# Sample rows through one transpose, the first weight chunk ordered by feature block, one product that spreads a norm's sums

## The chip, the cores and the metric

One core of a Trainium2 chip runs the whole kernel. The metric is the device time of one execution in microseconds (us), as the median of several runs.

## The reference

One decoder layer with 2048 features runs over 264 tokens: 256 of a prompt and one new token for each of eight samples. Everything is float32. In outline, with the details of the three branches left out:

```
xn = rmsnorm(x, norm_mix_g)                      # x * rsqrt(mean(x*x) + eps) * g
z  = xn @ w_in                                   # 2048 x 9728: gmlp, q, k, v, memory q, gates
o_g, o_a, o_m = gmlp(z), window_attention(z), memory_attention(z, mem_prompt)
merged = sum over b of sigmoid(gate_b) * (o_b @ w_br_b)
x = x + merged @ w_out
h = rmsnorm(x, norm_ffn_g) @ w_up                # 2048 x 11264
h = conv_b + sum over j of shifted h * conv_w[j]
x = x + (gelu(a) * b) @ w_down                   # a, b = the halves of h
y = rmsnorm(x, final_norm_g)
```

The change lies in the first step (x to xn, and the first product of it) and in the two places where a norm's 1/rms is worked out.

## The kernel before

**Layout.** Tokens lie along the free axis, features on the 128 partitions, so x is turned once on arrival: `xT`, 16 feature blocks of 128 x 264. A float32 operand is held as two parts of type float32r, a rounded one and the rest: `xhi` and `xlo` for x (with the gain, and without 1/rms, which is multiplied in when a product leaves PSUM), `whi` and `wlo` for the weights. One block of a product takes three matmuls (hi hi, lo hi, hi lo).

**The stream.** `gemm` writes chunks into one list. A chunk is two feature blocks of one product: its load fills `raw` (four buffers), `split` makes `whi` on ScalarE (ACT) and `wlo` on VectorE (DVE), and TensorE (PE) then does nm blocks x 2 feature blocks x 3 matmuls. `run` writes `split` ahead of use: chunk 0 alone first, then chunks 1 and 2 ahead of the matmuls of chunk 1, then one more chunk each time, and again two (5 and 6) ahead of chunk 4's. Every engine issues strictly in the order in which the code is written (`InOrder`). A slot is the work of one output block; `later(n, f)` writes f into the stream n slots on.

**x.** x arrives in eight column groups `xl`, each with two feature blocks. I call these pairs 0 to 7, and pair k feeds chunk k of the first product, q's first half (nm = 3, 18 matmuls a chunk). `x_parts(k0)` turns a pair with PE into PSUM tiles named `xtp`: four transposes of 128 x 128 and two small ones of the sample rows `xs`. ACT then writes both `xhi` and DVE both `xlo`. `x_kept` copies block one of the pair to `xT` on ACT and block two on DVE, squares them (ACT and GpSimd, called POOL), and POOL adds the squares to `ssum`. Each `xtp` before the change holds one feature block, in a PSUM tile of its own. In chunk k the pair k+1 is turned after the first output block; only pair 1 is turned ahead of chunk 0.

**Norms.** `token_norm` sums `ssum` over the partitions token by token (six small PE instructions, `ntp`), and `spread` brings 1/rms to all partitions with a product of a diagonal (`stp`). This happens for x (`r_bc`) and for the feed-forward part (`r2_bc`).

`mem_prep`, which the change leaves alone, turns two blocks of the memory rows into one PSUM tile `mtp`; ACT writes `mhi` from it and DVE `mlo`. PSUM tiles come from `psA` (`acc_t`, 4 buffers) and `psM` (`mis_t`, 4 buffers), each buffer 128 x 512 float32.

Of the kernel before, what the change touches and what calls it, by code (L numbers as in the profile page):

```python
# [39 lines left out]
class InOrder:  # L40
    """An engine whose instructions issue in the order in which they are written."""
# [19 lines left out]
def body(ctx, tc, x_prompt, x_sample, cache_swa_k, cache_swa_v, cache_mem_k, cache_mem_v, state_conv,  # L61
# [21 lines left out]
    # ---- slots: a slot is the matrix work of one output block and weight chunk; other work is  # L83
    # written into the stream at a slot, far enough behind what it needs ----
# [19 lines left out]
    def inv_sqrt(dst, v, shape):  # L104
        """Stages of dst = 1 / sqrt(v), with a step of Newton's method."""
        y = sm.tile(shape, F32, name="rs_y", tag="rs_y%d" % shape[1], bufs=2)
        t = sm.tile(shape, F32, name="rs_t", tag="rs_t%d" % shape[1], bufs=2)

        def a():
            S.activation(y, v, AF.Sqrt)  # L110

        def b():
            V.reciprocal(y, y)
            V.scalar_tensor_tensor(out=t, in0=y, scalar=-0.5, in1=y, op0=mul_, op1=mul_)
            V.tensor_tensor(t, t, v, op=mul_)
            V.scalar_tensor_tensor(out=dst, in0=t, scalar=1.5, in1=y, op0=add_, op1=mul_)
        return a, b

    def token_norm(srcs, out):
        """Stages of out[token] = 1 / rms over the features, from sums of squares over the blocks."""  # L120
        st = {}

        def a():
            tp = st["tp"] = mis_t("ntp")
            for tb in range(3):
                np_ = 128 if tb < 2 else 8
                for i, q in enumerate(srcs):
                    T.matmul(tp[:np_, tb:tb + 1], lhsT=q[:, 128 * tb:128 * tb + np_], rhs=ones[:, 0:1],
                             start=i == 0, stop=i == len(srcs) - 1)
            v = st["v"] = sm.tile([128, 3], F32, name="nv_", tag="nv_", bufs=2)  # L130
            G.memset(v, 1.0)

        def b():
            tp, v = st["tp"], st["v"]
            V.tensor_scalar(v[:, 0:2], tp[:, 0:2], 1.0 / D, EPS, op0=mul_, op1=add_)
            V.tensor_scalar(v[:8, 2:3], tp[:8, 2:3], 1.0 / D, EPS, op0=mul_, op1=add_)
            st["f"] = inv_sqrt(out, v, [128, 3])
            st["f"][0]()
        return a, b, lambda: st["f"][1]()

    def spread(r, dst):
        """Stages of dst[p, token] = r[token] for every partition p."""
        st = {}

        def a():
            dg = st["dg"] = sm.tile([128, NT], F32, name="dg", tag="sq", bufs=4)
            V.tensor_scalar(dg[:, 0:128], ident, r[:, 0:1], None, op0=mul_)
            V.tensor_scalar(dg[:, 128:256], ident, r[:, 1:2], None, op0=mul_)
            V.tensor_scalar(dg[:8, 256:264], ident[:8, :8], r[:8, 2:3], None, op0=mul_)

        def b():
# [7 lines left out]
    ident = cst.tile([128, 128], F32, name="ident")  # L159
    make_identity(nc, ident)  # L160
    ones = cst.tile([128, 128], F32, name="ones")
    G.memset(ones, 1.0)
# [12 lines left out]
    rx = cst.tile([128, 3], F32, name="rx")  # L175
# [6 lines left out]
    st_ld, st_mix, st_pb, st_me, st_gt, st_s2, st_s2p, st_s3k, st_s3v, st_s1, st_s5, st_mg = (  # L182
        ExitStack() for _ in range(12))

# [1 line left out]
    ld = st_ld.enter_context(tc.tile_pool(name="ld", bufs=1))  # L186
    xls = [ld.tile([128, 2, 256], F32, name="xl%d" % i) for i in range(8)]
    xs = ld.tile([8, D], F32, name="xs")
    gm = ld.tile([16, 128], F32, name="gm")
    grow = ld.tile([48, 128], F32, name="grow")  # L190

    def x_load(i):
        Y.dma_start(xls[i], x_prompt[0, :, 256 * i:256 * i + 256].rearrange("(t p) f -> p t f", p=128))
        if i == 0:
            Y.dma_start(gm, norm_mix_g[0].rearrange("(k p) -> k p", p=128))
            Y.dma_start(xs, x_sample[:, 0, :])
# [3 lines left out]

    def x_parts(k0):
        """Two feature blocks of x, gained and split."""
        if k0 == 0:
            tp = mis_t("gtp")
            T.transpose(out=tp[:, 0:16], in_=gm, identity=ident[:16, :16])
            V.tensor_copy(gT[:, 0:16], tp[:, 0:16])
        xl = xls[k0 // 2]
        tps = []
        for j in range(2):
            kb = k0 + j  # L210
            tp = mis_t("xtp")
            js = slice(128 * j, 128 * j + 128)
            T.transpose(out=tp[:, 0:128], in_=xl[:, 0, js], identity=ident)
            T.transpose(out=tp[:, 128:256], in_=xl[:, 1, js], identity=ident)
            T.transpose(out=tp[:, 256:264], in_=xs[:, 128 * kb:128 * kb + 128], identity=ident[:8, :8])
            tps.append(tp[:, :NT])
        for j in range(2):
            S.activation(xhi[:, k0 + j, :], tps[j], AF.Copy, scale=gT[:, k0 + j:k0 + j + 1])
        for j in range(2):
            V.scalar_tensor_tensor(out=xlo[:, k0 + j, :], in0=tps[j], scalar=gT[:, k0 + j:k0 + j + 1],  # L220
                                   in1=xhi[:, k0 + j, :], op0=mul_, op1=sub_)
        return tps

    def x_kept(k0, tps):
        S.copy(xT[:, k0, :], tps[0])
        V.tensor_copy(xT[:, k0 + 1, :], tps[1])
        sq = [sm.tile([128, NT], F32, name="sq", tag="sq", bufs=4) if k0 + j else ssum for j in range(2)]
        S.activation(sq[0], tps[0], AF.Square)
        if k0 < KB - 2:
            G.tensor_tensor(sq[1], xT[:, k0 + 1, :], xT[:, k0 + 1, :], op=mul_)  # L230
# [3 lines left out]
        if k0:  # L234
            E.tensor_tensor(ssum, ssum, sq[0], op=add_)
        E.tensor_tensor(ssum, ssum, sq[1], op=add_)
# [16 lines left out]
    def split(load, n, pairs):  # L253
# [13 lines left out]
        for r, h, l in vs:  # L267
            V.tensor_tensor(l, r, h, op=sub_)
        return list(zip(his, los))
# [28 lines left out]
    def gemm(load, nkb, nm, ab, evac, pairs=False, pre=None, mid=None, banks=None):  # L298
        """ab() gives the high and low parts of the moving operand."""
        st = {}  # L300

        def chunk(kc):
            def mm(ws):
# [4 lines left out]
                ahi, alo = ab()  # L308
                for m in range(nm):
                    o = st["acc"][m][:, :NT]  # L310
                    for j in range(2):
                        kb = 2 * kc + j
                        hi, lo = blk(ws[j][0], m), blk(ws[j][1], m)
# [1220 lines left out]
```

## Time and profile before

| | |
|---|---|
| median of 3 runs | 1548.16 us (1545.2 to 1552.09) |
| span of the profiled execution | 1546.5 us, mean granted TensorE clock 0.997 |
| PE busy | 1531.6 us, 99% |
| DVE, ACT, POOL busy | 1011.2, 768.9, 139.3 us |
| DMA | 285.57 MB, 185 GB/s |

The span runs from the first to the last instruction of one profiled execution. The profile gives no time of that execution beside its span; the span lies 1.7 us under the median of the runs. Over the whole kernel PE is busy nearly all the time, but the change touches the first 55 us and two short places later, so these have to be read by themselves.

### The profile page before, as it was taken

How to read it: one execution, taken by the hardware profiler on the slowest of the kernel's cores; microseconds unless marked ns; L12 is line 12 of the kernel's file. 1: busy time of each engine (PE TensorE's matmuls, PEld its weight loads, DVE VectorE, ACT ScalarE, POOL GpSimd, SP SyncE). 2: the span in 40 equal slices, each digit the busy share in tenths (PEclk: the TensorE clock that was granted, in tenths of full speed). 3: DMA queues.
4: the chain of work that ended last, by engine and by line, in shares of the span. 5: the costliest groups of instructions: out<-in, count | busy, mean ns of one | idle time of the engine just before them, and what ended most of it. 6: DMA issues, size and time to landing. Idle time of an engine off the chain costs nothing.

```text
span 1546.5 us, 31609 instructions
## 1 busy us (share of the span) xinstructions
PE 1531.6 (99%) x12203; PEld 1497.4 (97%) x12203; DVE 1011.2 (65%) x1934; ACT 768.9 (50%) x1492; POOL 139.3 (9%) x215
## 2 busy tenths in 40 slices
PE   9999999999999999999999999999999999999997
PEld 8987899999999999999999999999999999999997
DVE  7577678867475555765667777776444776777564
ACT  6467644565444444445555555554343555555443
POOL 5022042400000000001100000000000000001110
PEclk9999999999999999999999999999999999999998
DMA  6754498665666565555566666655556666665743
GB/s 198 213 179 153 137 309 299 219 188 159 181 182 183 180 179 180 185 172 185 178 178 179 186 182 178 180 184 182 178 180 181 185 177 179 181 184 174 185 162 111
DMA packets 154372, 285.57 MB, mean 185 GB/s; under 512 B 11509, under 2 KB 29357, under 8 KB 154165
## 3 DMA queue, kind: packets, MB, share of 16 engines
q1 hardware_dynamic: 152444, 278.14, 58.8%
q0 software_dynamic: 1776, 5.41, 1.5%
q8 instruction: 96, 1.57, 0.4%
q14 instruction: 56, 0.45, 0.1%
HBM read 279.10 MB, written 6.82 MB: 185 GB/s over the span
## 4 chain that ended last, share of the span: by engine, by line
PE 96%; DVE 1%; DMA 1%; issue 0%; ACT 0%; POOL 0%; DVEq 0%; SPq 0%; ACTq 0%; POOLq 0%
PE acc L50 88%; PE macc L50 3%; DMA raw<-in_w_down_dram 1%; PE sps L50 1%; PE ov L50 1%; DVE wlo L50 1%; PE xtp L50 1%; PE acc__552 L50 0%; PE acc__551 L50 0%; PE ssp L50 0%; PE ytp L50 0%; PE ptp L50 0%; PE mtp L50 0%; PE msov L50 0%; DMA gm<-in_norm_mix_g_dram 0%
## 5 line engine op out<-in xcount | busy, mean ns | idle before, releaser
L50 DVE TENSOR_TENSOR wlo<-raw,whi 128x512 fp32r<-128x512 f32 (+1 forms) x1008 | 658.9, 695 | 478.0 <-ACT whi L50 477.5
L50 ACT CAST whi<-raw 128x512 fp32r<-128x512 f32 (+1 forms) x1008 | 564.8, 607 | 618.5 <-PE acc L50 421.7
L50 PE MATMUL acc<-xg_hi,whi 128*128 128x264 f32 x1408 | 400.4, 284 | 0.0
L50 PE MATMUL acc<-xg_lo,whi 128*128 128x264 f32 x1408 | 400.2, 284 | 0.0
L50 PE MATMUL acc<-xg_hi,wlo 128*128 128x264 f32 x1408 | 400.1, 284 | 0.0
L50 PE MATMUL acc<-xhi,whi 128*128 128x264 f32 x1152 | 336.9, 292 | 0.0
L50 PE MATMUL acc<-xlo,whi 128*128 128x264 f32 x1152 | 328.3, 285 | 0.4 <-DVE xlo L50 0.4
L50 PE MATMUL acc<-xhi,wlo 128*128 128x264 f32 x1152 | 327.9, 285 | 0.0
L50 PEld LDWEIGHTS acc<-xg_hi,whi 128*128 128x128 f32 x1408 | 265.5, 189 | 0.0
L50 PEld LDWEIGHTS acc<-xg_lo,whi 128*128 128x128 f32 x1408 | 265.0, 188 | 0.0
L50 PEld LDWEIGHTS acc<-xg_hi,wlo 128*128 128x128 f32 x1408 | 264.4, 188 | 0.0
L50 PEld LDWEIGHTS acc<-xhi,whi 128*128 128x128 f32 x1152 | 217.9, 189 | 4.5 <-issue 3.1
L50 PEld LDWEIGHTS acc<-xlo,whi 128*128 128x128 f32 x1152 | 217.7, 189 | 1.2 <-DVE xlo L50 0.6
L50 PEld LDWEIGHTS acc<-xhi,wlo 128*128 128x128 f32 x1152 | 217.1, 188 | 0.0
L50 PE MATMUL acc<-ahi,whi 128*128 128x264 f32 x704 | 201.1, 286 | 0.9 <-DVE xT L50 0.9
L50 PE MATMUL acc<-alo,whi 128*128 128x264 f32 x704 | 200.1, 284 | 0.0
L50 PE MATMUL acc<-ahi,wlo 128*128 128x264 f32 x704 | 200.0, 284 | 0.0
L50 PEld LDWEIGHTS acc<-ahi,whi 128*128 128x128 f32 x704 | 132.7, 189 | 1.4 <-issue 1.0
L50 PEld LDWEIGHTS acc<-alo,whi 128*128 128x128 f32 x704 | 132.6, 188 | 0.0
L50 PEld LDWEIGHTS acc<-ahi,wlo 128*128 128x128 f32 x704 | 132.2, 188 | 0.0
L50 DVE SCALAR_TENSOR_TENSOR t<-H,cvT,t 128x256 f32<-128x256 f32 x176 | 84.7, 481 | 3.1
L50 POOL TENSOR_TENSOR ssum<-ssum,sq 128x264 f32<-128x264 f32 x41 | 35.7, 870 | 476.8 <-ACT sq L50 454.4
(336 smaller groups left out, 1724.9 us busy)
## 6 DMA issues: line engine op xcount, KB each, us to landing
raw<-in_w_up_dram SPq DMA_DIRECT2D x176, 512.0 KB
raw<-in_w_in_dram SPq DMA_DIRECT2D x112, 512.0 KB
raw<-in_w_down_dram SPq DMA_DIRECT2D x88, 512.0 KB
raw<-in_w_in_dram SPq DMA_DIRECT2D x48, 384.0 KB
raw<-in_w_out_dram SPq DMA_DIRECT2D x32, 512.0 KB
raw<-in_w_mem_kv_dram SPq DMA_DIRECT2D x16, 512.0 KB
raw<-in_w_br_g_dram SPq DMA_DIRECT2D x12, 512.0 KB
raw<-in_w_br_a_dram SPq DMA_DIRECT2D x48, 128.0 KB
```

Source lines behind the costliest of these rows:

```text
L50: r = f(*a, **k)
```

## The change

It does six things.

1. The eight sample rows are loaded as 128 rows of 128 features (16 for each sample) and turned by one transpose, together with the gain rows in another (`xstp`); the 16 small transposes in the pairs go. The sample columns of `xhi`, `xlo` and `xT` are written for all 16 blocks at once, and the other writes are 256 wide in place of 264.
2. Both blocks of a pair now go into one PSUM tile `xtp`, 256 columns each.
3. Chunk 0 does block one of its pair for all three outputs first; pair 1 is turned after that and one more output, not ahead of the chunk. `xhi` of block 1 of pair 0 is written by DVE.
4. `xs` and the gains are loaded from ACT's queue; SP's begins with x and the weights. Eleven filler products `wake` in place of eight, six ahead of the first transposes and five behind.
5. A norm's sums come out on all partitions from one product of `ones` with `ssum`; square root, reciprocal and Newton's step then run on 128 x 264. `spread` and its two products go.
6. The load buffers of x lie on the other side of SBUF.

```diff
-    def token_norm(srcs, out):
+    def token_norm(src, dst):
         st = {}
         def a():
             tp = st["tp"] = mis_t("ntp")
-            for tb in range(3):
-                np_ = 128 if tb < 2 else 8
-                for i, q in enumerate(srcs):
-                    T.matmul(tp[:np_, tb:tb + 1], lhsT=q[:, 128 * tb:128 * tb + np_], rhs=ones[:, 0:1],
-                             start=i == 0, stop=i == len(srcs) - 1)
...
+            T.matmul(tp[:, :NT], lhsT=ones, rhs=src, start=True, stop=True)
         def b():
-            tp, v = st["tp"], st["v"]
-            V.tensor_scalar(v[:, 0:2], tp[:, 0:2], 1.0 / D, EPS, op0=mul_, op1=add_)
-            V.tensor_scalar(v[:8, 2:3], tp[:8, 2:3], 1.0 / D, EPS, op0=mul_, op1=add_)
-            st["f"] = inv_sqrt(out, v, [128, 3])
-            st["f"][0]()
-        return a, b, lambda: st["f"][1]()
-    def spread(r, dst):
...
+            v = st["v"] = sm.tile([128, NT], F32, name="nvb", tag="sq", bufs=4)
+            V.tensor_scalar(v, st["tp"][:, :NT], 1.0 / D, EPS, op0=mul_, op1=add_)
+            S.activation(dst, v, AF.Sqrt)
+        def c():
+            y = st["y"] = sm.tile([128, NT], F32, name="nyb", tag="sq", bufs=4)
+            V.reciprocal(y, dst)
+        def d():
+            v, y = st["v"], st["y"]
+            V.scalar_tensor_tensor(out=dst, in0=y, scalar=-0.5, in1=y, op0=mul_, op1=mul_)
+            V.tensor_tensor(v, dst, v, op=mul_)
+            V.scalar_tensor_tensor(out=dst, in0=v, scalar=1.5, in1=y, op0=add_, op1=mul_)
+        return a, b, c, d
...
+    ld = st_ld.enter_context(tc.tile_pool(name="ld", bufs=1, side="right"))
+    xls = [ld.tile([128, 2, 256], F32, name="xl%d" % i) for i in range(8)]
+    xs = ld.tile([128, 128], F32, name="xs")
+    gm = ld.tile([128, 128], F32, name="gm")
...
+    S.dma_start(xs, x_sample.rearrange("b o (k f) -> (b o k) f", f=128))
+    S.dma_start(gm[0:16, :], norm_mix_g[0].rearrange("(k p) -> k p", p=128))
...
-            Y.dma_start(gm, norm_mix_g[0].rearrange("(k p) -> k p", p=128))
-            Y.dma_start(xs, x_sample[:, 0, :])
...
+    def x_first():
+        tx = mis_t("xstp")
+        T.transpose(out=tx[:, 0:128], in_=xs, identity=ident)
+        T.transpose(out=tx[:, 128:256], in_=gm, identity=ident)
+        tp = mis_t("xtp")
+        tps = [tp[:, 256 * j:256 * j + 256] for j in range(2)]
+        for j in range(2):
+            for t in range(2):
+                T.transpose(out=tps[j][:, 128 * t:128 * t + 128], in_=xls[0][:, t, 128 * j:128 * j + 128], identity=ident)
+        rows = tx[:, 0:128].rearrange("p (b k) -> p k b", k=KB)
+        gx = sm.tile([128, KB, NS], F32, name="gx", bufs=1)
+        V.tensor_copy(gT[:, 0:16], tx[:, 128:144])
+        V.tensor_tensor(gx, rows, gT[:, 0:16].unsqueeze(2).to_broadcast([128, KB, NS]), op=mul_)
+        S.activation(xhi[:, 0, NP_], tps[0], AF.Copy, scale=gT[:, 0:1])
+        S.copy(xhi[:, :, NS_], gx)
+        V.tensor_scalar(xhi[:, 1, NP_], tps[1], gT[:, 1:2], None, op0=mul_)
+        V.scalar_tensor_tensor(out=xlo[:, 0, NP_], in0=tps[0], scalar=gT[:, 0:1], in1=xhi[:, 0, NP_],
+                               op0=mul_, op1=sub_)
+        V.tensor_tensor(xlo[:, :, NS_], gx, xhi[:, :, NS_], op=sub_)
+        def second():
+            V.scalar_tensor_tensor(out=xlo[:, 1, NP_], in0=tps[1], scalar=gT[:, 1:2], in1=xhi[:, 1, NP_],
+                                   op0=mul_, op1=sub_)
+        def kept():
+            x_kept(0, tps)
+            V.tensor_copy(xT[:, :, NS_], rows)
+            G.tensor_tensor(gx, xT[:, :, NS_], xT[:, :, NS_], op=mul_)
+            later(4, lambda: V.reduce_sum(ssum[:, NS_], gx.rearrange("p k b -> p b k"), axis=AX.X))
+        return second, kept
...
+        tp = mis_t("xtp")
+        tps = [tp[:, 256 * j:256 * j + 256] for j in range(2)]
-            tp = mis_t("xtp")
             js = slice(128 * j, 128 * j + 128)
-            T.transpose(out=tp[:, 0:128], in_=xl[:, 0, js], identity=ident)
-            T.transpose(out=tp[:, 128:256], in_=xl[:, 1, js], identity=ident)
-            T.transpose(out=tp[:, 256:264], in_=xs[:, 128 * kb:128 * kb + 128], identity=ident[:8, :8])
-            tps.append(tp[:, :NT])
+            for t in range(2):
+                T.transpose(out=tps[j][:, 128 * t:128 * t + 128], in_=xl[:, t, js], identity=ident)
         for j in range(2):
...
-                    wake = mis_t("wake")
+                    x_load(0)
+                    wake = acc_t("wake")
+                    for _ in range(6):
+                        T.matmul(wake[:, 0:128], lhsT=ones, rhs=ones, start=True, stop=True)
+                    second, held["x"] = x_first()
                     for _ in range(5):
                         T.matmul(wake[:, 0:128], lhsT=ones, rhs=ones, start=True, stop=True)
-                    x_load(0)
-                    held["x"] = x_parts(0)
-                    for _ in range(3):
-                        T.matmul(wake[:, 0:128], lhsT=ones, rhs=ones, start=True, stop=True)
-                ws[chunks[nxt]] = split(*items[chunks[nxt]][0])
+                    ws[chunks[0]] = split(*items[chunks[0]][0], between=second)
+                else:
+                    ws[chunks[nxt]] = split(*items[chunks[nxt]][0])
...
+                early = lead and kc == 0
+                if early:
+                    for m in range(nm):
+                        three(m, 0)
...
+                    for j in range(early, 2):
+                        three(m, j)
...
-    def pre_q0(kc):
+    def mid_q0(kc):
         if kc == 0:
-            x_kept(0, held.pop("x"))
-            x_pair(2)
+            tps = x_parts(2)
+            held.pop("x")()
+            x_kept(2, tps)
+        else:
+            x_pair(2 * kc + 2)
...
-        a, b, c = token_norm([ssum], rx)
-        d, e = spread(rx, r_bc)
-        later(1, a)
-        later(2, b)
-        later(5, c)
-        later(5, d)
-        later(8, e)
+        for f, n in zip(token_norm(ssum, r_bc), (1, 2, 4, 6)):
+            later(n, f)
```

What the code leaves to the order of writing shows in the built programs.

The first rows of DVE in the steady part of x, before the change: one pair (two `xlo`, one copy to `xT`) and the weights of one chunk. The names in brackets are what an instruction waits for.

```order
L50 SCALAR_TENSOR_TENSOR xlo<-xtp,gT,xhi 128x264 [waits Activation_49] x2
L50 COPY xT<-xtp 128x264
L50 TENSOR_TENSOR wlo<-raw,whi 128x2x3x64 [waits DMAHW3_49,DVE_49,Activation_49]
L50 TENSOR_TENSOR wlo<-raw,whi 128x2x3x64 [waits DVE_49,Activation_49]
L50 SCALAR_TENSOR_TENSOR xlo<-xtp,gT,xhi 128x264 [waits Activation_49] x2
```

The same place on DVE in the changed program.

```order
L50 SCALAR_TENSOR_TENSOR xlo<-xtp,gT,xhi 128x256 [waits PE_49,Activation_49]
L50 SCALAR_TENSOR_TENSOR xlo<-xtp,gT,xhi 128x256
L50 COPY xT<-xtp 128x256 [waits Activation_49]
L50 TENSOR_TENSOR wlo<-raw,whi 128x2x3x64 [waits DMAHW3_49,DVE_49,Activation_49]
L50 TENSOR_TENSOR wlo<-raw,whi 128x2x3x64 [waits DVE_49,Activation_49]
```

Each `xlo` waited for its own `xhi`; now the first one carries the wait for both, and the copy to `xT`, which waited for nothing, waits for ACT.

ACT at that place before: two `xhi`, the copy and the square of one pair, then the weights.

```order
L50 ACTIVATE xhi<-xtp,gT 128x264 [waits PE_49] x2
L50 COPY xT<-xtp 128x264 [waits DVE_49]
L50 ACTIVATE sq<-xtp 128x264 [waits Pool_49]
L50 CAST whi<-raw 128x2x3x64 [waits DMAHW3_49,Activation_49]
L50 CAST whi<-raw 128x2x3x64 [waits Activation_49]
```

And in the changed program.

```order
L50 ACTIVATE xhi<-xtp,gT 128x256 [waits PE_49]
L50 ACTIVATE xhi<-xtp,gT 128x256
L50 COPY xT<-xtp 128x256 [waits DVE_49]
L50 ACTIVATE sq<-xtp 128x256 [waits DVE_49,Pool_49]
L50 CAST whi<-raw 128x2x3x64 [waits DMAHW3_49,Activation_49]
L50 CAST whi<-raw 128x2x3x64 [waits Activation_49]
```

The square now waits for DVE too, and the weight casts stand behind it. In the built program the copy on ACT waits for the count that DVE's second `xlo` raises, DVE's copy for ACT's copy, and the square for DVE's copy.

PE from the start, before the change.

```order
L50 MATMUL wake<-ones 128x128 x5
L50 MATMUL gtp<-ident,gm 128x16
L50 MATMUL xtp<-ident,xl_99 128x128 x2
L50 MATMUL xtp<-ident,xs 128x8
L50 MATMUL xtp<-ident,xl_99 128x128 x2
L50 MATMUL xtp<-ident,xs 128x8
L50 MATMUL wake<-ones 128x128 x3
L50 MATMUL xtp<-ident,xl_100 128x128 x2
L50 MATMUL xtp<-ident,xs 128x8
L50 MATMUL xtp<-ident,xl_100 128x128 x2
L50 MATMUL xtp<-ident,xs 128x8
L50 MATMUL acc<-xhi,whi 128x264
```

And now, up to the first product.

```order
L50 MATMUL wake<-ones 128x128 x6
L50 MATMUL xstp<-ident,xs 128x128
L50 MATMUL xstp<-ident,gm 128x128
L50 MATMUL xtp<-ident,xl_76 128x128 x4
L50 MATMUL wake<-ones 128x128 x5
L50 MATMUL acc<-xhi,whi 128x264
```

The transposes of pair 1 (`xl_100` before) have left the place ahead of the first product; twelve products now stand ahead of them.

## Rows read from the trace of the kernel before

**Rows 1.** The page: span, busy time by engine, shares of the chain that ended last.
```profile
span 1546.5 us, 31609 instructions
...
PE 1531.6 (99%) x12203; PEld 1497.4 (97%) x12203; DVE 1011.2 (65%) x1934; ACT 768.9 (50%) x1492; POOL 139.3 (9%) x215
...
PE 96%; DVE 1%; DMA 1%; issue 0%; ACT 0%; POOL 0%; DVEq 0%; SPq 0%; ACTq 0%; POOLq 0%
```
**Rows 2.** Timeline, PE, 0 to 14 us: start, length, instruction, [idle before, releaser].
```profile
4.35 0.26 PE L50 MATMUL gtp<-ident,gm 16*128 16x16 f32 x1 [0.64 <-DMA gm<-in_norm_mix_g_dram]
...
6.18 1.65 PE L50 MATMUL wake<-ones 128*128 128x128 f32 x6
...
9.21 0.59 PE L50 MATMUL acc<-xhi,whi 128*128 128x264 f32 x1
9.59 0.42 PE L50 MATMUL acc<-xlo,whi 128*128 128x264 f32 x1
9.81 0.42 PE L50 MATMUL acc<-xhi,wlo 128*128 128x264 f32 x1
...
12.56 0.28 PE L50 MATMUL acc<-xhi,whi 128*128 128x264 f32 x1
12.68 0.28 PE L50 MATMUL acc<-xlo,whi 128*128 128x264 f32 x1
```
**Rows 3.** Timeline, PE, 26.7 to 32 us.
```profile
26.75 0.39 PE L50 MATMUL acc<-xlo,whi 128*128 128x264 f32 x1 [0.43 <-DVE xlo L50]
...
30.80 0.38 PE L50 MATMUL xtp<-ident,xl 128*128 128x128 f32 x2
...
31.79 0.39 PE L50 MATMUL acc<-xhi,whi 128*128 128x264 f32 x1
```
**Rows 4.** Timeline, DVE, 9 to 50 us.
```profile
9.01 0.49 DVE L50 SCALAR_TENSOR_TENSOR xlo<-xtp,gT,xhi 128x264 fp32r<-128x264 f32 x1 [0.44 <-ACT xhi L50]
...
26.22 0.88 DVE L50 SCALAR_TENSOR_TENSOR xlo<-xtp,gT,xhi 128x264 fp32r<-128x264 f32 x2
27.02 0.42 DVE L50 COPY xT<-xtp 128x264 f32<-128x264 f32 x1
27.84 1.74 DVE L50 TENSOR_TENSOR wlo<-raw,whi 128x384 fp32r<-128x384 f32 x2 [0.40 <-ACT whi L50]
29.51 0.88 DVE L50 SCALAR_TENSOR_TENSOR xlo<-xtp,gT,xhi 128x264 fp32r<-128x264 f32 x2
...
32.80 0.88 DVE L50 SCALAR_TENSOR_TENSOR xlo<-xtp,gT,xhi 128x264 fp32r<-128x264 f32 x2
...
48.74 1.03 DVE L50 TENSOR_TENSOR wlo<-raw,whi 128x384 fp32r<-128x384 f32 x2 [1.16 <-ACT whi L50]
```
**Rows 5.** Timeline, ACT, 26 to 28 us, and one row of POOL.
```profile
26.73 0.38 ACT L50 COPY xT<-xtp 128x264 f32<-128x264 f32 x1 [1.66 <-DVE xlo L50]
27.01 0.40 ACT L50 ACTIVATE sq<-xtp 128x264 f32<-128x264 f32 x1
27.29 0.92 ACT L50 CAST whi<-raw 128x384 fp32r<-128x384 f32 x2
...
28.10 2.10 POOL L50 TENSOR_TENSOR ssum<-ssum,sq 128x264 f32<-128x264 f32 x2
```
**Rows 6.** Timeline, 118 to 121 us: memory rows, two blocks in one `mis` tile.
```profile
118.89 0.66 PE L50 MATMUL mtp<-ident,ml 128*128 128x128 f32 x4
119.30 0.48 PE L50 MATMUL macc<-whi,mhi 128*128 128x512 f32 x1
...
119.58 0.84 ACT L50 ACTIVATE mhi<-mtp,gT 128x256 fp32r<-128x256 f32 x2 [0.77 <-PE mtp L50]
...
120.46 0.87 DVE L50 SCALAR_TENSOR_TENSOR mlo<-mtp,gT,mhi 128x256 fp32r<-128x256 f32 x2 [0.92 <-ACT mhi L50]
```
**Rows 7.** Timeline, PE: matmuls of the first of two norms.
```profile
36.28 0.63 PE L50 MATMUL ntp<-ones,ssum 128*128 128x1 f32 x6
...
42.04 0.91 PE L50 MATMUL stp<-dg,ones 128*128 128x256 f32 x4
```

More of the change, by code (lines that the diff above doesn't have):

```diff
@@ new lines, in token_norm @@
+        return a, b, c, d
+    st_ld = ExitStack()
+    ld = st_ld.enter_context(tc.tile_pool(name="ld", bufs=1, side="right"))
+    xls = [ld.tile([128, 2, 256], F32, name="xl%d" % i) for i in range(8)]
+    xs = ld.tile([128, 128], F32, name="xs")
+    gm = ld.tile([128, 128], F32, name="gm")
+    grow = ld.tile([48, 128], F32, name="grow")
+    ones = cst.tile([128, 128], F32, name="ones")
+    G.memset(ones, 1.0)
+    G.memset(gm, 0.0)
+    S.dma_start(xs, x_sample.rearrange("b o (k f) -> (b o k) f", f=128))
@@ L181, in body @@
     R, M, held = {}, {}, {}
[L182 to L190, printed above, removed]
+    st_mix, st_pb, st_me, st_gt, st_s2, st_s2p, st_s3k, st_s3v, st_s1, st_s5, st_mg = (
+        ExitStack() for _ in range(11))
+    NP_ = slice(0, NP)
+    NS_ = slice(NP, NT)
     def x_load(i):
         Y.dma_start(xls[i], x_prompt[0, :, 256 * i:256 * i + 256].rearrange("(t p) f -> p t f", p=128))
-        if i == 0:
-            Y.dma_start(gm, norm_mix_g[0].rearrange("(k p) -> k p", p=128))
-            Y.dma_start(xs, x_sample[:, 0, :])
         if i == 7:
@@ L217, in x_parts @@
         for j in range(2):
-            S.activation(xhi[:, k0 + j, :], tps[j], AF.Copy, scale=gT[:, k0 + j:k0 + j + 1])
+            S.activation(xhi[:, k0 + j, NP_], tps[j], AF.Copy, scale=gT[:, k0 + j:k0 + j + 1])
         for j in range(2):
-            V.scalar_tensor_tensor(out=xlo[:, k0 + j, :], in0=tps[j], scalar=gT[:, k0 + j:k0 + j + 1],
-                                   in1=xhi[:, k0 + j, :], op0=mul_, op1=sub_)
+            V.scalar_tensor_tensor(out=xlo[:, k0 + j, NP_], in0=tps[j], scalar=gT[:, k0 + j:k0 + j + 1],
+                                   in1=xhi[:, k0 + j, NP_], op0=mul_, op1=sub_)
@@ L222, in x_parts @@
         return tps
     def x_kept(k0, tps):
-        S.copy(xT[:, k0, :], tps[0])
-        V.tensor_copy(xT[:, k0 + 1, :], tps[1])
-        sq = [sm.tile([128, NT], F32, name="sq", tag="sq", bufs=4) if k0 + j else ssum for j in range(2)]
+        S.copy(xT[:, k0, NP_], tps[0])
+        V.tensor_copy(xT[:, k0 + 1, NP_], tps[1])
+        sq = [sm.tile([128, NT], F32, name="sq", tag="sq", bufs=4)[:, NP_] if k0 + j else ssum[:, NP_]
+              for j in range(2)]
         S.activation(sq[0], tps[0], AF.Square)
@@ L251, in act, with split @@
         items.append((None, fn))
-    def split(load, n, pairs):
+    def split(load, n, pairs, between=None):
         raw = wp.tile([128, 2, 512], F32, name="raw", tag="raw", bufs=4)
@@ L268, in split @@
             V.tensor_tensor(l, r, h, op=sub_)
+            if between and r is vs[0][0]:
+                between()
         return list(zip(his, los))
@@ L296, in blk, with gemm @@
         return t[:, 128 * m:128 * m + 128]
-    def gemm(load, nkb, nm, ab, evac, pairs=False, pre=None, mid=None, banks=None):
+    def gemm(load, nkb, nm, ab, evac, pairs=False, pre=None, mid=None, banks=None, lead=False):
         st = {}
```

48 lines of the change are left out of this document (11 added, 37 removed).

## The prediction

> **What bounds the kernel now.** I read the page first, then the first 55 us engine by engine in the timeline, because nearly all the edits lie there. Over the whole kernel PE is busy 99% and 96% of the chain that ended last is PE [rows 1]. So whatever moves PE's stream early on moves the end by the same amount; behind the first 55 us nothing in the change gives time back but the second norm.
>
> The first stretch has other limits, one after the other. PE waits for the gain rows until 4.35 us and starts the first product at 9.21 [rows 2]. The first matmuls stand 0.22 us apart, later ones 0.12 [rows 2]: the two clock levels, 1.2 and 2.4 GHz, with the rise before 12.56. From about 23 us PE no longer sets the pace of x: one of its matmuls waits for DVE's `xlo` [rows 3], and DVE runs the same round from 26.22 to 29.51 and on to 32.80, 3.29 us each [rows 4]. In such a round DVE has two `xlo`, one copy, an idle 0.40 us until ACT's cast, and two `wlo`. The two `wlo` take 1.67 us from start to start of the next (27.84 to 29.51) while POOL adds squares [rows 4, 5]; later, with POOL quiet, the same two take 1.03 [rows 4]. PE's own work in a round is 18 x 0.12 = 2.2 us and 0.99 for turning a pair (30.80 to 31.79) [rows 3], 3.2 in all. So PE and the ACT-DVE round are about equally long today, and cutting PE's share alone can't shorten a round.
>
> **The change part by part.**
>
> *One PSUM tile for a pair.* This is the edit that I think decides. ACT and DVE both read `xtp` several times. The trace shows what happens when two blocks share a tile: ACT's two `mhi` run from 119.58 to 120.42, and DVE's first `mlo`, which waits for ACT, starts at 120.46, behind both [rows 6]. With a tile for each block, today, DVE's part of block one overlaps ACT's of block two. The Trainium skill, PSUM — Partial Sum Buffer, section on PSUM bank collisions, says that two engines must not touch one bank at once, two reads included, and that software has to keep them apart. By that rule the program must make ACT and DVE take turns on the shared tile; the rows of the memory blocks agree (0.04 us between the engines' turns), and so do the waits in the changed order.
>
> So a round becomes one line of turns. Two `xlo` 0.87 (as the two `mlo`) [rows 6]; ACT's copy 0.38 [rows 5]; DVE's copy 0.42 [rows 4]; from the start of ACT's square to DVE's first `wlo` 0.83 (27.01 to 27.84, the square and one cast) [rows 4, 5]; two `wlo` 1.67; three more handovers of 0.04. That is 4.29 us against 3.29: 1.0 us more for each pair. POOL's square and sums, 2.10 us for the sums alone [rows 5], start behind DVE's copy, so the `wlo` still meet them and I leave 1.67. PE needs 2.2 us and four transposes of 0.41 (as 118.89 to 119.30) [rows 6], 2.6 in all: hidden under 4.29. The cover also swallows the saving on the small transposes: 0.58 us a pair on PE that nobody waits for any more.
>
> There are six rounds from `xlo` of pair 1 to `xlo` of pair 7, today 9.01 to 32.80, 23.79 us [rows 4]. Four are as above. The first carries the weights of two chunks and pair 0's copies, which moved there from ahead of the chunk: 0.87, ACT 0.38, DVE 0.42, ACT's square and next copy 0.66, DVE 0.42, 0.83, then four `wlo` at 0.84 beside POOL (3.34), handovers 0.2: 7.1 us. The copy of the sample rows on DVE, not in the trace, lies beside ACT's 0.66; between nothing and a wide copy's 0.42 it stays under. The fourth carries two chunks as well: 2.62 up to the weights, two `wlo` 1.67, two when POOL is through 0.96 (1.03 less the overlap): 5.25. Sum 7.1 + 4 x 4.29 + 5.25 = 29.5, so **+5.7 us**.
>
> *The start.* The gains are still the second small load of a queue, so I keep 4.35 us as the start of the transposes. Five or six transposes at 0.22 to 0.28 each (six `wake` instructions take 1.65) [rows 2] end near 5.7. Then five `wake`, ten instructions, 2.4 us at the lower level: first product at about 8.0, against 9.21. By then ACT has written `xhi`, the sample rows and the first `whi`, and DVE the first `wlo`, so PE does not wait there. But pair 1, which used to be turned ahead of the chunk, comes behind twelve products: 2.6 us at 0.22. Turned by 11.6, both `xhi` 0.84, so `xlo` of pair 1 starts at 12.5, against 9.01. Were the clock up from the `wake` on, this would be 10.3: first product at 7.0, the third held for `wlo` until 7.6, twelve at 0.12, transposes 0.41, `xhi` 0.9. Bounds +1.3 and +3.5; PE is busy without a break from 4.35 rather than from 6.18, so the rise should come earlier than today, and I take the middle, **+2.5**. The new loads on ACT stand ahead of a table load that is done long before the first `xhi`; SP's weights go out sooner by the two loads that left its queue, and the first products wait for PE, not for them.
>
> *The norms.* The sums cost PE 0.63 and the spreading 0.91 [rows 7]. The new product is the wide half of the latter, 0.91 less two narrow instructions at 0.105 (0.63 / 6): 0.70. Saved 0.84, twice, **-1.7 us**; PE sets the pace in both places. The reciprocal over 264 columns has no row. It lies between a pass of that width (0.42) and, at the far end, several; ahead of `r_bc`'s first use there are four slots of six matmuls, 2.9 us, and behind it in DVE's queue only weights that are needed a chunk later. I cost it at nothing; if it took over 3 us, the q outputs would come late, into PSUM buffers wanted a chunk later still.
>
> *The rest* (other side of SBUF, `wake` in another PSUM buffer) moves no wait that the trace shows: 0.
>
> Sum: 2.5 + 5.7 - 1.7 = **+6.5 us**. From the profiled span of 1546.5 that is 1553.0. The span lies 1.7 under the median of the runs, so a median of 1554.7 us, 0.42% over the 1548.16 of before. A measurement of this kernel tells about 0.5% (7.7 us) from no change, so this is just inside it: bounds 1555.9 and 1540.4.
>
> **The rivals.**
>
> *The clock falls back.* In the long rounds PE would work 2.6 of 4.29 us and idle for the rest; behind chunk 0, in the first round, it would idle longest. At the lower level a round needs 22 x 0.22 = 4.84 us of PE, more than the turns take, and PE would set the pace: 0.55 x 6 = 3.3 us more, 1558.0. For it: the first 12 us show that PE with gaps stays low. Against it: at 0.22 PE is full, and full is what raised the clock before 12.56, so it could only swing. It decides as soon as more than half the rounds run low. The Trainium skill, TensorE: Matmul & The Clock Gate, section on HAM oscillation, says that a product engine which pauses between groups can be throttled again for every group. No row of before shows it, as PE has no long gap there behind 12.56.
>
> *The turns cost nothing.* Were the waits met by work already done, a round would stay at 3.29, the two double ones at 4.96 (two more `wlo`, 1.67): 23.1 us, 0.7 less than today. With 2.5 - 1.7 that is +0.1, a median of 1548.3. Against it: DVE is the one who is late today, and each turn lies on its line.
>
> *PE sets the pace.* If rounds fell to PE's 2.6 us, the gain would be 1.2 us at the first product, 7 x 0.58 for the pairs and 1.7 for the norms, 7.0 us: 1541.2. It would need DVE's round under 2.6, and it is 3.29 already.
>
> **How the numbers follow.** The sum as worked out 0.55 (its own range 1552.5 to 1557), the clock 0.25, no cost of turns 0.15, PE's pace 0.05. Slower by over 0.5% comes from nine tenths of the clock's share and a third of the first (start at its upper bound): 0.42. Faster by over 0.5%: half of the last, 0.03. Within: 0.55. The range leaves out PE's pace, the lower half of the third case, and the clock held low throughout with a late start: 1549 to 1560.
>
> **What would show it.** DVE's first `xlo` of a pair starting behind both `xhi`; ACT's copy and square each with idle time ended by DVE; rounds of 4.3 us on DVE; PE idle over a microsecond in each, ended by DVE's `xlo`; spacing of 0.12 there, or 0.22 if the clock rival is right. First product near 8 us, `xlo` of pair 1 between 10 and 12.5, the new `ntp` about 0.7 long. The forecast is wrong if the turns overlap, if POOL's squares end sooner in the longer rounds and let `wlo` run at 1.0, or if a delay of the first 55 us is made up later.

## The result, and the profile after

The changed kernel takes 1557.45 us (median of 4 runs, 1556.05 to 1558.09), the kernel before, run beside it, 1548.55 (1545.2 to 1552.09). The ratio is 1.0056, with a 95% interval of 1.0045 to 1.0068: slower by 8.9 us, where 6.5 was forecast. The time lies inside the range given; the loss is just beyond the 0.5% mark, which the interval still includes, and the forecast time of 1554.7 lay just inside it.

The page of the changed kernel, span and engines (before: [rows 1]):

```profile
span 1554.3 us, 31566 instructions
...
PE 1530.4 (98%) x12178; PEld 1497.8 (96%) x12178; DVE 1016.8 (65%) x1929; ACT 768.4 (49%) x1492; POOL 138.9 (9%) x215
```

PE's busy time fell by 1.2 us while the span grew by 7.8: the loss is idle time of PE. It lies early. The timeline of PE in the changed kernel (start, length, instruction, [idle before, releaser]):

```profile
7.06 0.37 PE L50 MATMUL acc<-xhi,whi 128*128 128x264 f32 x1
...
8.08 0.28 PE L50 MATMUL acc<-xhi,whi 128*128 128x264 f32 x1
8.20 0.28 PE L50 MATMUL acc<-xlo,whi 128*128 128x264 f32 x1
...
9.16 0.60 PE L50 MATMUL xtp<-ident,xl 128*128 128x128 f32 x4
...
13.88 0.59 PE L50 MATMUL acc<-xhi,whi 128*128 128x264 f32 x1 [3.40 <-ACT whi L50]
...
31.34 0.39 PE L50 MATMUL acc<-xhi,whi 128*128 128x264 f32 x1 [0.95 <-ACT xhi L50]
32.98 0.39 PE L50 MATMUL acc<-xlo,whi 128*128 128x264 f32 x1 [1.26 <-DVE xlo L50]
...
44.82 0.64 PE L50 MATMUL ntp<-ssum,ones 128*128 128x264 f32 x2
45.10 0.48 PE L50 MATMUL acc__538<-xhi,whi 128*128 128x264 f32 x1
```

The first product is 2.15 us earlier than in [rows 2], the matmuls are 0.12 apart already at 8.08, and the chunk is through by 10.5. Then PE waits 3.40 us in one piece. The clock had risen at 6.6 us, by the trace's record of it, against 12.4 before. DVE in the changed kernel, the first round, the start of the second, and the last round in full:

```profile
10.66 0.88 DVE L50 SCALAR_TENSOR_TENSOR xlo<-xtp,gT,xhi 128x256 fp32r<-128x256 f32 x2 [2.01 <-ACT xhi L50]
...
13.86 3.33 DVE L50 TENSOR_TENSOR wlo<-raw,whi 128x384 fp32r<-128x384 f32 x4 [0.85 <-ACT whi L50]
18.12 0.88 DVE L50 SCALAR_TENSOR_TENSOR xlo<-xtp,gT,xhi 128x256 fp32r<-128x256 f32 x2 [0.94 <-ACT xhi L50]
...
36.91 0.86 DVE L50 SCALAR_TENSOR_TENSOR xlo<-xtp,gT,xhi 128x256 fp32r<-128x256 f32 x2
38.21 0.42 DVE L50 COPY xT<-xtp 128x256 f32<-128x256 f32 x1 [0.44 <-ACT xT L50]
39.55 1.89 DVE L50 TENSOR_TENSOR wlo<-raw,whi 128x384 fp32r<-128x384 f32 x2 [0.91 <-ACT whi L50]
41.36 0.86 DVE L50 SCALAR_TENSOR_TENSOR xlo<-xtp,gT,xhi 128x256 fp32r<-128x256 f32 x2
```

ACT in the changed kernel, one row of the first round and then the last round:

```profile
10.52 0.37 ACT L50 COPY xT<-xtp 128x256 f32<-128x256 f32 x1
...
37.81 0.37 ACT L50 COPY xT<-xtp 128x256 f32<-128x256 f32 x1 [1.59 <-DVE xlo L50]
38.73 0.38 ACT L50 ACTIVATE sq<-xtp 128x256 f32<-128x256 f32 x1 [0.55 <-DVE xT L50]
39.01 0.92 ACT L50 CAST whi<-raw 128x384 fp32r<-128x384 f32 x2
```

Read the last round of the two together: `xlo` ends at 37.77, ACT's copy starts at 37.81, DVE's copy at 38.21, ACT's square at 38.73. No two of these reads of `xtp` overlap, each step's idle time is ended by the other engine, and a round takes 41.36 - 36.91 = 4.45 us against 3.29 [rows 4]. PE's clock in the changed kernel, by windows (stretch, its length, PE's busy time, then granted clock, DMA share and GB/s):

```profile
14.00:20.00 6.00, 5.92 (x24) 0.50 0.49 137
20.00:34.00 14.00, 10.21 (x75) 0.99 0.38 116
34.00:36.00 2.00, 2.00 (x11) 0.50 0.68 237
```

The clock falls back twice, to 1.2 GHz (0.50), first behind the 3.40 us wait, and again at about 34 us, behind a round with two waits of 0.95 and 1.26 us.

Four places add up the early loss against the kernel before:

| | before | after | difference |
|---|---|---|---|
| `xlo` of pair 1 starts | 9.01 | 10.66 | +1.65 |
| six rounds, to `xlo` of pair 7 | 23.79 | 30.70 | +6.91 |
| from there to `kstp`, the first transposes behind the norm and the in-projections | 49.17 | 48.00 | -1.17 |
| `kstp` starts | 81.97 | 89.36 | +7.39 |

These are single traces, so it matters what of them repeats. Of the runs below, the new norm alone (two traces) has the early code of the kernel before, the idle products (two traces) that of the changed kernel, and the filler that of the changed kernel up to the end of chunk 0. `xlo` of pair 1 starts 3.54 us behind ACT's first `xhi` in all traces with the old early code and 4.91 to 4.96 behind it in all with the new; the first `xhi` itself, which waits for loads and the transposes behind them, moves between 5.4 and 6.8 us. The six rounds take 30.7 us in every trace of the changed code, but 24.7 and 24.6 in the two further ones of the old, where the clock rose at 14.6 and 14.2 us. Counted from the first `xhi`, and with the norm's gain allowed for, `kstp` is therefore 6.2 to 7.1 us later, and the trace of before in the table is the quickest of its code.

### The profile page after: what moved, and what is told of

Read it like the earlier page. It is cut to its first block, busy times and chain, and to the rows that moved or that the text cites. A ratio compares the mean times of both kernels' runs of the same rounds, so it can differ in the third digit from the quotient of the medians.

```text
span 1554.3 us, 31566 instructions
## 1 busy us (share of the span) xinstructions
PE 1530.4 (98%) x12178; PEld 1497.8 (96%) x12178; DVE 1016.8 (65%) x1929; ACT 768.4 (49%) x1492; POOL 138.9 (9%) x215
## 4 chain that ended last, share of the span: by engine, by line
PE 83%; DVE 1%; issue 0%; ACT 0%; POOLq 0%; DVEq 0%; POOL 0%; ACTq 0%
PE acc L50 81%; PE ytp L50 0%; PE mov L50 0%; PE msp L50 0%; PE msov L50 0%; DVE wlo L50 0%; PE sov L50 0%; PE mps L50 0%; PE vgtp L50 0%; DVE y_tm L50 0%; PE mptp L50 0%; DVE ys_tm L50 0%; PE nt L50 0%; DVE vlo L50 0%; DVE den L50 0%
## 5 line engine op out<-in xcount | busy, mean ns | idle before, releaser
L50 POOL TENSOR_TENSOR ssum<-ssum,sq 128x264 f32<-128x264 f32 (+1 forms) x41 | 34.6, 843 | 476.1 <-ACT sq L50 474.2
```

Source lines behind the costliest of these rows:

```text
L50: r = f(*a, **k)
```

## Experiments

All times below are medians with the kernel before run on the same chip beside them: 1549.17 for the first group (two tiles, old order, filler, one copy), 1548.9 for the second (norm only, two tiles with the old order, idle products), 1548.82 for the third (late copies, norm again).

**The theory and its rivals.** *Turns*: on the shared tile every read of ACT and DVE stands in one line between `xlo` and the next chunk's weights, which lengthens each round. *Clock*: PE idles, falls to 1.2 GHz and becomes the pace. *Order*: pair 1 comes too late behind chunk 0.

**A tile for each block** (the copy of the sample rows moves, so that a fourth `mis` buffer is free):

```diff
-        tp = mis_t("xtp")
-        tps = [tp[:, 256 * j:256 * j + 256] for j in range(2)]
+        tps = [mis_t("xtp")[:, 0:256] for j in range(2)]
```

> The changed kernel with each feature block of a pair in a PSUM tile of its own again; the sample rows are copied to xT a little earlier so that their tile comes free. Theory (the turns on one shared tile are the loss): DVE's rounds fall from 4.45 us to about 3.3, from the first xlo of pair 1 to that of pair 7 about 24 us in place of 30.7, and the median falls by 6 to 7.5 us against the changed kernel, to about the time of before or up to 2 us under it. Rival (TensorE's clock falls back in the gaps and the lower level is the loss): with shorter rounds the gaps close too, so this run alone would also gain, but the gain would show in spacing of the products, not in the handovers. Rival (the new order of chunk 0 is the loss): under 2 us gained.

Measured 1548.20, ratio 0.9995 (0.9987 to 1.0004): the whole loss is gone. The same round in this kernel, DVE and then ACT:

```profile
30.46 0.86 DVE L50 SCALAR_TENSOR_TENSOR xlo<-xtp,gT,xhi 128x256 fp32r<-128x256 f32 x2
31.25 0.41 DVE L50 COPY xT<-xtp 128x256 f32<-128x256 f32 x1
32.06 1.72 DVE L50 TENSOR_TENSOR wlo<-raw,whi 128x384 fp32r<-128x384 f32 x2 [0.40 <-ACT whi L50]
```
```profile
30.97 0.37 ACT L50 COPY xT<-xtp 128x256 f32<-128x256 f32 x1 [1.04 <-DVE xlo L50]
31.24 0.39 ACT L50 ACTIVATE sq<-xtp 128x256 f32<-128x256 f32 x1
```

ACT copies at 30.97, inside DVE's two `xlo`, and the round is 3.24 us. PE also waits only 1.47 us ahead of chunk 1 here, and the clock stays at 2.4 GHz. Of the 1.21 us that a steady round loses, 1.04 lie between `xlo` and the first `wlo` (1.60 us here, 2.64 in the changed kernel), where the turns stand, and 0.17 in the `wlo`. This run takes away the turns and the low clock together; the next ones part them.

**Filler for the clock**: 15 more `wake` products in front of chunk 1, the shared tile kept.

```diff
+    def fill_q0(kc):
+        if kc == 1:
+            for _ in range(15):
+                T.matmul(held["wake"][:, 0:128], lhsT=ones, rhs=ones, start=True, stop=True)
```

> The changed kernel with 15 filler products behind chunk 0, where TensorE idles 3.4 us and its clock falls. Theory (turns): the first round shortens by at most 1 us (7.46 to about 6.6, as the pair's transposes and six products run at the upper level), the others stay at 4.45; median 0 to 1 us lower. Rival (clock is the loss): the spacing of 0.22 us at 14 to 20 us and at 34 to 37 us goes, and 3 us or more are gained.

Measured 1554.17, ratio 1.0031 (1.0020 to 1.0043). The filler fills the gap, and the matmuls behind it stand 0.12 to 0.13 apart, where the changed kernel has 0.22. The second fall of the clock came in this run too, as the last row shows. PE in this kernel, and one window (stretch, length, busy time, clock, DMA share, GB/s):

```profile
10.43 3.51 PE L50 MATMUL wake<-ones 128*128 128x128 f32 x30
...
17.66 0.28 PE L50 MATMUL acc<-xhi,whi 128*128 128x264 f32 x1
17.78 0.28 PE L50 MATMUL acc<-xlo,whi 128*128 128x264 f32 x1
```
```profile
34.00:36.00 2.00, 2.00 (x11) 0.50 0.45 158
```

The first round falls from 7.46 to 6.85 us, the later ones stay at 4.4 to 4.5. So the first fall of the clock cost 0.6 us up to pair 7. The second cost nothing there: in the run with 20 idle products below, whose early code is the changed kernel's, the clock stayed at 1.00 between 34 and 38 us, and that round took 4.47 us, against 4.45 in the changed kernel. The rest of the longer rounds is left to the turns. The run gained 3.3 us, though; where the other 2.7 come from is taken up below.

**Old order of chunk 0**, shared tile kept: pair 0's copies and pair 1's transposes ahead of the chunk's products.

```diff
+    def pre_q0(kc):
+        if kc == 0:
+            held.pop("x")()
+            x_pair(2)
-         mid=mid_q0, lead=True
+         pre=pre_q0, mid=lambda kc: kc and x_pair(2 * kc + 2)
```

> The changed kernel (shared tile kept) with pair 1 turned ahead of chunk 0 again and chunk 0 in its old order of output blocks. Theory (turns): rounds stay at 4.4 to 4.5 us and the median stays 4 us or more above before; only the start and the first round move, by 1 to 3 us either way. Rival (order of chunk 0 is the loss): most of the 8.9 us comes back, median within 3 us of before.

Measured 1557.21, ratio 1.0051 (1.0039 to 1.0064): no difference to the changed kernel that the runs could show. But **the old order with a tile for each block**, the same edit on the first experiment, is another matter.

> The changed kernel with a tile for each block (as in the run with two tiles, 1548.2 us) and the old order of chunk 0, with the second pair's transposes ahead of its products. If the order is worth nothing, as with the shared tile (1557.2 against 1557.4), this stays within 0.7 us of 1548.2. If the shared tile only hid its price, the second pair's xlo starts earlier than the 10.95 us of the two tiles' run, by up to the 1.2 us that the twelve products of chunk 0 ahead of its transposes take, and the time falls to about 1547.0. If the new order helps where the turns are gone, the first acc product starts later and the time rises by as much.

Measured 1546.81, ratio 0.9986 (0.9978 to 0.9995), 1.4 under the two tiles with the new order; the two intervals overlap, so by the medians alone this could be noise. The traces are clearer: `xlo` of pair 1 starts at 9.31 instead of 10.95, and `kstp` at 80.02 instead of 81.68, 1.6 us each time, with the first `xhi` at 5.9 in both. With the shared tile the old order saves less. Counted from the first `xhi` (5.75 in the changed kernel, 6.22 in this trace), `xlo` of pair 1 comes 0.4 us earlier than in the changed kernel, where with two tiles it is 1.7. ACT says why. First the old order with the shared tile, then with two:

```profile
8.70 0.37 ACT L50 COPY xT<-xtp 128x256 f32<-128x256 f32 x1 [0.99 <-DVE xlo L50]
9.56 0.38 ACT L50 ACTIVATE ssum<-xtp 128x256 f32<-128x256 f32 x1 [0.49 <-DVE xT L50]
9.84 0.83 ACT L50 ACTIVATE xhi<-xtp,gT 128x256 fp32r<-128x256 f32 x2
```
```profile
7.55 0.39 ACT L50 ACTIVATE ssum<-xtp 128x256 f32<-128x256 f32 x1
8.80 0.84 ACT L50 ACTIVATE xhi<-xtp,gT 128x256 fp32r<-128x256 f32 x2 [0.86 <-PE xtp L50]
```

In the first, pair 0's two waits for a turn (0.99 and 0.49) stand in ACT's queue ahead of pair 1's `xhi`, which start at 9.84 though pair 1 was turned by 7.7. In the second, ACT is through early and waits for PE.

**One copy for both blocks**: the tile stays shared, DVE copies its 512 columns at once, POOL squares from `xT`, and ACT reads the tile only for `xhi`.

```diff
-        S.copy(xT[:, k0, NP_], tps[0])
-        V.tensor_copy(xT[:, k0 + 1, NP_], tps[1])
+        V.tensor_copy(xT[:, k0:k0 + 2, NP_], whole[k0])
-        S.activation(sq[0], tps[0], AF.Square)
+            G.tensor_tensor(sq[0], xT[:, k0, NP_], xT[:, k0, NP_], op=mul_)
```

> The changed kernel, shared tile kept, but with one turn in place of four: DVE copies both blocks to xT in one instruction behind its xlo, and the squares are made from xT, on POOL (the last pair's on ScalarE). Theory (it is the turns on DVE's line, not the sharing as such): rounds of 3.2 to 3.6 us, median 5 to 7 us under the changed kernel. Rival (a shared tile is slow in itself, or the clock): rounds stay above 4 us.

Measured 1550.46, ratio 1.0012 (1.0004 to 1.0021). Late rounds are 2.8 and 3.2 us (`xlo` at 29.89, 32.67, 35.90); the first is still 6.3 with the clock at 0.72 of full between 14 and 20 us. Fewer turns give back most of the loss with the tile still shared. The edit also takes a copy and a square off ACT, though, so not all of the gain need be the turns.

**Copies behind the weights**: the shared tile, the old order, and a pair's copies and squares written behind the next chunk's weights. All turns are kept; only their place in the queues changes.

```diff
         if kc == 0:
             held.pop("x")()
-            x_pair(2)
+            turn(2)
+        elif kc < KB // 2:
+            x_kept(2 * kc, held.pop(("p", 2 * kc)))
+    def turn(k0):
+        if k0 < KB:
+            held["p", k0] = x_parts(k0)
```

> The changed kernel with its shared tile, the old order of chunk 0 (1557.2 us), and the copies and squares of a pair written behind the next chunk's weights. If the shared tile costs only by the turns that stand between xlo and the next weights (theory of the turns), those turns now lie beside the two wlo, VectorE's round is 0.87 + 1.67 + 0.42 = 3.0 us against 4.45, and six rounds give back 6 to 9 us: about 1549, near the kernel with two tiles. If sharing a tile costs as such, wherever the reads stand, the rounds stay near 4.3 us and the time near 1557.

Measured 1547.38, ratio 0.9989 (0.9980 to 0.9998), 9.8 us under the same kernel with the copies in their old place. DVE in this kernel:

```profile
29.50 0.88 DVE L50 SCALAR_TENSOR_TENSOR xlo<-xtp,gT,xhi 128x256 fp32r<-128x256 f32 x2 [1.24 <-ACT xhi L50]
30.29 1.05 DVE L50 TENSOR_TENSOR wlo<-raw,whi 128x384 fp32r<-128x384 f32 x2
31.26 0.41 DVE L50 COPY xT<-xtp 128x256 f32<-128x256 f32 x1
...
32.91 0.88 DVE L50 SCALAR_TENSOR_TENSOR xlo<-xtp,gT,xhi 128x256 fp32r<-128x256 f32 x2 [1.24 <-ACT xhi L50]
```
```profile
31.76 0.38 ACT L50 ACTIVATE sq<-xtp 128x256 f32<-128x256 f32 x1 [0.98 <-DVE xT L50]
32.04 0.83 ACT L50 ACTIVATE xhi<-xtp,gT 128x256 fp32r<-128x256 f32 x2
```

The second fence is ACT. The turns are still there, and something still waits behind them: ACT's square waits for DVE's copy, the next pair's `xhi` stand behind the square, and DVE idles 1.24 us for them in every round. The round is 3.41 us all the same, for two reasons that come with the new place. The first `wlo` starts 0.79 us behind `xlo`, not 2.64. And the `wlo` run between POOL's sums instead of beside them, two in 1.05 us instead of 1.89, which alone is 0.84 of the 1.04 us that a round loses. No run parts the two. Up to `kstp` the gain is 7.6 of the 9.8 us (81.34 against 88.90). **The same with a tile for each block** is the fastest kernel of the study.

> The kernel with a tile for each block and the old order (1546.8 us) with the copies to xT and the squares of a pair written behind the next chunk's weights instead of ahead of them. If VectorE's line sets the round there (two xlo 0.8, xT 0.4, an idle 0.4 until ACT's cast, two wlo 1.65: 3.25), the idle 0.4 goes and each of six rounds falls to about 2.85, 2.4 us in all: 1544.4. If TensorE's own 2.6 us a round and the weights' arrival set it by then, the rounds stay above 3.1 and the time within 1 us of 1546.8.

Measured 1544.63, ratio 0.9974 (0.9964 to 0.9983), faster than both kernels. Its steady rounds are 3.15 us, not the 2.85 expected: the idle 0.40 went, but the two `wlo` take 2.0 us there beside POOL. That the time met the 1544.4 expected is luck: the six rounds did lose 2.3 us, but 1.3 of them in the first.

**The new norm alone**, on the kernel before; no diff is shown, as it is `token_norm` of the change and nothing else. It was run twice.

> The kernel before with one part of the change alone: the norm sums spread by one product, in both norms. If the saving seen in the changed kernel's trace holds (the new product costs TensorE's row of starts 0.28 us where the small products and the spread together cost 1.39, twice in the program) and all of it reaches the end, the time falls by 2 x 1.11 = 2.2 us, to a ratio of about 0.9986. If VectorE's longer work (the reciprocal alone 1.79 us) sits on a path that sets the end, or TensorE's saved time is waited away behind a later transfer, nothing is gained: 0.9995 to 1.0005.

> The kernel before with the new norm alone once more, as one of its twelve runs was 9 us longer (clock 0.991) and widened the interval. If both norms' saving reaches the end, the ratio is about 0.9986; if half is taken up by waits in the middle, 0.9992, as the other eleven runs had it; if none, 0.9995 to 1.0005.

Measured 1547.77 with ratio 0.9996 (0.9985 to 1.0007), and 1547.69 with 1.0000 (0.9985 to 1.0015): inconclusive by the interval, because 3 of the 24 runs took 1556 to 1558 us, with a clock of 0.99. Both medians are 1.1 us under before, half of the 2.2 that both norms would give. In the first trace `xlo` of pair 7 is 1.17 us later than before and `kstp` stands at 81.97 in both, so the first norm gives PE 1.17 us. What the long runs are, the second trace shows; PE in it:

```profile
242.65 0.64 PE L50 MATMUL pnbc<-pnb,ones 1*128 1x128 f32 x2 [1.40 <-DVE pnb L50]
243.22 0.59 PE L50 MATMUL acc<-xhi,whi 128*128 128x264 f32 x1
```

and by windows of 10 us (busy times of PE, PEld, DVE, ACT, POOL, then granted clock, DMA share and GB/s):

```profile
240.00:250.00 10.00, 8.60 (x42) 8.04 (x42) 7.13 (x17) 1.95 (x4) 2.87 (x4) 0.64 0.85 308
250.00:260.00 10.00, 10.00 (x48) 10.00 (x48) 3.20 (x6) 1.02 (x2) 0.00 (x0) 0.50 0.49 156
260.00:270.00 10.00, 10.00 (x82) 9.86 (x81) 6.76 (x18) 5.09 (x14) 0.30 (x2) 1.00 0.50 138
```

Behind one wait of 1.40 us the clock is at 1.2 GHz until about 260: `mktp`, at 181 us, starts 0.4 us earlier than before, `sttp`, at 256 us, 10.2 later. In the kernel before that `pnbc` has no wait in the trace.

**Idle products at 89 us**, ahead of the `kstp` transposes of the changed kernel, 20 and then 40, to see how much of a known delay reaches the end.

```diff
             tp = mis_t("kstp")
+            for _ in range(20):
+                T.matmul(tp[:, 0:128], lhsT=ones, rhs=ones, start=True, stop=True)
```

> The changed kernel with 20 idle products of 128x128 on TensorE just ahead of the kstp transposes, at 89 us, where TensorE is busy without a gap. They delay what follows by about 20 x 0.11 = 2.2 us. If time lost early reaches the end one for one, the median is 1557.4 + 2.2 = 1559.6. If the middle of the program takes up or adds to a delay by how its waits fall, the end moves by another amount, by over 1 us more or less.

> As the run with 20 idle products at 89 us, with 40: a delay of about 4.4 us. One for one the median is 1561.8. If the middle takes up or adds to delays, the three kernels with 0, 20 and 40 do not lie on a line: their steps differ by over 1 us from 2.2 each.

Measured 1560.92 (ratio 1.0079, 1.0067 to 1.0091) and 1564.65 (1.0103, 1.0088 to 1.0118). The expected delays were half of the real ones, since each product is two instructions. PE with 40 of them:

```profile
89.05 9.09 PE L50 MATMUL kstp<-ones 128*128 128x128 f32 x80
97.98 0.27 PE L50 MATMUL kstp<-ident,kvT 128*8 128x128 f32 x1
```

They delay PE by 8.93 us, 20 of them by half, 4.46. The medians moved by 3.5 and 7.2 (from 1557.45): 1.0 and 1.7 us less than the delay, which is not clear of noise, as each ratio is known to about 0.12% (1.9 us). In the traces, one each, PE's last matmul moves 0.8 and 0.3 us less than `kstp`. So the middle passes nearly all of a delay on.

## Why the prediction was right, step by step

**One PSUM tile for a pair.** Right, and shown: with two tiles the waits between the turns go and the whole loss with them, while the shared tile with the clock held up, or with the old order, keeps its long rounds. The round was forecast at 4.29 and is 4.45. By its terms: `xlo` to ACT's copy 0.90 (0.91 forecast), to DVE's copy 0.40 (0.42), to the square 0.52 (0.46), to the first `wlo` 0.82 (0.83), two `wlo` 1.81 (1.67). Nearly all of the 0.16 is the `wlo`, the term that was mis-sized. They lie beside POOL's two sums in both kernels, and the sums got shorter in turn, 1.74 against 2.10 [rows 5]; why the share shifts towards POOL was not tried. The fourth round is 5.39 (5.25 forecast). The Trainium skill, PSUM — Partial Sum Buffer, section on PSUM bank collisions, has the rule that ACT and DVE must not read one bank at once, and the trace agrees in that no two of their reads of a shared tile overlap, with 0.04 us between turns; what two reads at once would do, no run here shows. The late copies add that the price of the turns depends on what stands behind them.

**The first round** was forecast at 7.1 and is 7.46; with the clock held up by filler it is 6.85. That the two are near is partly luck. DVE's own line was shorter than forecast: ACT's copy of pair 0, priced as a turn of 0.38 us, is from another tile and runs beside `xlo` (10.52 against 10.66), and the four `wlo` are through at 17.19, 6.5 us behind `xlo`. PE at the lower clock, which the forecast left out, ends last instead: `xlo` of pair 2 waits 0.94 us for ACT's `xhi`, and those for PE's transposes. In sum the six rounds cost 6.9 us by these two traces, and 6.0 to 6.1 against the other two traces of the old code, where 5.7 were forecast.

**The start** was forecast at +2.5 with bounds of +1.3 and +3.5, and is +1.65. The mis-sized term is the clock: it was up by 8.08 us, as in the lower bound, so the twelve products took 2.1 us and the first began at 7.06 (7.0 in that bound). The reason given for an earlier rise does not hold, though, and neither does the remark that PE stays low with gaps: in the trace of before PE works without a break from 4.35 on as well (four rows from 4.54 to 5.98 stand between those in [rows 2]) and stays low until 12.4. Over all traces the rise came at 12.4 to 14.6 us with the old early code and at 4.7 to 9.6 with the new or in part new; why was not tried. Of the 1.65, 1.4 lie between the first `xhi` and `xlo` of pair 1 and 0.3 in the arrival of the loads. The new order is not the whole price: with the shared tile the turns of pair 0 hold ACT's `xhi` back in the old order too, which leaves 0.4 us to gain of 1.7.

**The norms** were forecast at -0.84 each. PE's trace gives more: the new product takes 0.28 us from its start to the next, and the early stretch as a whole gains 1.17, 1.17 to 1.22 in every kernel of the study without idle products there, but for the two with late copies, where `ntp` waits for the last sum. The second norm gives 1.15 in the traces. The forecast of 0.70 for the new product was a length, and the product is 0.64 long; but the next matmul starts 0.28 behind its start, and the distance between starts was what was wanted. The reciprocal, for which there was no row, takes 1.79 us over 264 columns and delays nothing, since `kstp` keeps its 1.17.

**The rivals.** *The clock falls back*: it did, twice, but at a price of 0.6 us in the rounds, not 3.3. In the rounds at 1.2 GHz behind the first, PE's work still fits under the turns, as the round from 32.46 to 36.91 shows, 4.45 us with the clock at 0.50 between 34 and 36. The Trainium skill, TensorE: Matmul & The Clock Gate, section on HAM oscillation, tells of a kernel in which the clock falls again at every wait for data. Here it did not: rounds with one pause of 1.14 or 1.15 us stayed at 2.4 GHz, and the round with two, 0.95 and 1.26, fell in the changed kernel and did not in the run with 20 idle products (0.94 and 1.25). *The turns cost nothing* and *PE sets the pace* fell with the first trace.

**From the early loss to the end.** Up to `kstp` the terms add up: 1.65 + 6.91 - 1.17 = 7.39. The second norm leaves 6.2 of that. But in the middle the changed kernel loses 1.2 us, all of it by 320 us, and another 0.5 behind 1530 us, so that the profiled spans differ by 7.8; the medians differ by 8.9. The forecast took the middle to pass delays on unchanged. It does not, quite. PE's waits between 95 and 1530 us, in the kernel before and then in the changed kernel (us in all, times, longest):

```profile
PE acc L50 <- DVE xT L50: 0.9, 1, 0.9
PE mptp L50 <- DVE p__3722 L50: 0.7, 1, 0.7
PE msov L50 <- DVE vlo L50: 0.7, 2, 0.4
```
```profile
PE ssp L50 <- DVE KT L50: 1.7, 2, 1.2
PE msov L50 <- DVE vlo L50: 0.8, 2, 0.6
PE acc L50 <- DVE xT L50: 0.8, 1, 0.8
PE sstp L50 <- DVE sS L50: 0.2, 1, 0.2
```

That is 2.3 us before and 3.5 after. The kernel with two tiles has the wait for `KT` too (1.6 us). These waits come and go between kernels with the same work: the filler's kernel and the one with the old order reach `kstp` at 88.86 and 88.90 and end 3.0 us apart by medians, 3.5 by traces. In the filler's trace the waits are 2.1 us and in the other 4.0; 2.3 us of the difference arise between 290 and 320 us and 1.3 at about 1449. What shifts them was not settled. It bounds any such sum at about 3 us on this kernel.

So the mechanism was right, and the closeness of 6.5 to the measured loss is in part luck: by the traces the start was put 0.85 us too high, the rounds 1.2 too low, the norms 0.6 too low in what they save, and 1.7 us in the middle and at the end were not in the sum. Not tried by themselves were the one transpose for the sample rows, the loads from ACT's queue and the other side of SBUF.

## What to carry to other kernels

When two engines read a shared PSUM tile, write down the line of their turns and look at what stands behind it in either queue: here 1.0 us a round went to weights waiting behind copies that nobody needed yet, and moving the copies behind the weights gave back 9.8 us with the tile still shared, though much of that came from weights that then ran beside a quiet POOL. A reordering can measure as worthless beside a bigger limit and move the stream by 1.6 us once that is gone, so test the parts on both, and read what one trace says against a second trace of the same code. Price a matmul that others follow by the distance of starts, not by its length.

## What the runs showed of the hardware that was not expected

A single PE wait can cost many times its length: behind 1.40 us of waiting that ended at 242.65 us PE ran at 1.2 GHz for some 17 us and lost about 10. It does not always happen: PE waited 1.47 us in one piece in the kernel with two tiles and stayed at 2.4 GHz; it waited 2.29 us and two short pieces in the one with the old order and the shared tile, and the clock fell. Two `wlo` of 128x384 take 1.05 us where POOL is quiet and 1.9 beside its sums; so where POOL's work falls is worth up to 0.9 us a round here.
